# Moving the transposes, loads and sums of a seven-product matmul to other places in its written order

## The chip, the cores and the metric

The kernel runs on one core of a Trainium2 chip. The metric is device time in microseconds (us) of one execution, the median of several runs. One more execution is recorded by the hardware profiler; every duration below comes from that one.

## The reference

`x` has 8 x 1024 rows of 768 numbers. Each row is divided by its root mean square, scaled by `gamma`, and multiplied with a 768 x 2304 weight:

```python
rms = np.sqrt(np.mean(x ** 2, axis=-1, keepdims=True) + eps)
x_norm = x / rms * gamma
return np.matmul(x_norm, w_qkv).astype(np.float32)
```

## The kernel before

The 8192 rows are 64 tiles of 128 rows, called t. The first four tiles (t = 0 to 3) go through a plain bf16 matmul (`mm`, 512 columns at a time) while the weight is still arriving. The other 60 tiles form 30 pairs p = 2 to 31 (t = 2p and 2p+1). A pair is computed with a seven-product scheme in place of eight: the pair's rows and the two halves of the 768 inner numbers make a 2 x 2 of blocks (a11, a12, a21, a22), the weight is cut the same way (b11 to b22) in three column pieces c = 0, 1, 2 of twice 384 columns, and seven block products per piece, of sums and differences of blocks, give the four result blocks. A product (`product`) is three matmuls of 128 x 128 by 128 x 384.

For each tile there is a fixed chain of steps:

- `load_x`: the sync engine (SP) issues the load of 384 KB into one of 10 buffers.
- `pstat`, `prms`: ScalarE (ACT) squares and sums the row, then takes the root. `precip`: VectorE (DVE) takes the reciprocal.
- `pcast`: DVE scales the tile and writes it as f16 (line 626), into one of 6 buffers.
- `pxbar`: SP issues a DMA that transposes the f16 tile into one of 10 buffers `xT` (line 630).
- `osum`: four sums of blocks per pair (line 644), written to one tile `su` of a pool of three buffers. From pair 15 on they are all on GpSimd (POOL). A block of `su` is the stationary operand of four of the seven products.
- `product` on TensorE (PE, line 664), then `hold` (ACT or DVE, lines 671 and 673) copies a partial result from PSUM, `join` (DVE, line 680) adds a partial result to PSUM and writes an output block, `last` (ACT, line 684) writes the fourth output block.
- `rstore`: SP issues the store of one finished output row tile of 1152 KB (line 516).

Nothing is scheduled by a compiler. Each step gets a time, all steps are sorted by it, and they are emitted in that order; an engine executes its own steps strictly in the emitted order, each waiting only for the data and the buffers that it needs. The times therefore set only the order. SP has one queue for loads, transposes and stores alike, so a store that waits for its last `last` holds up the transposes behind it.

The order has two parts. The head is a list written out by hand or by a search (`PLAN`, 959 entries, pairs 2 to 14 and the plain matmuls); its times come from a planner's costs. The regular part (pairs 15 to 31) is a loop: `z` is the time of the pair's first product of a piece, and each step stands at `z + u * SLOT`, where `SLOT` is the time of one product (0.4875 us) and a pair takes 21 of these steps. Here a step of the beat is always such a slot; a negative `u` lies ahead of the pair's first product.

Of the kernel before, what the change touches and what calls it, by code (L numbers as in the profile page):

```python
# [15 lines left out]
HEAD_END = 164.41  # L16
# [11 lines left out]
    (10.183, "mm", 1, 0, "4"), (12.005, "conv", 1, 2, "POOL"), (12.006, "load_w", 7), (12.007, "load_w", 5),  # L28
    (12.008, "conv", 0, 1, "DVE"), (12.009, "mm", 0, 0, "5"), (12.010, "bound", 0, 1, "ACT"),
    (12.011, "mm", 0, 0, "4"), (12.012, "mm", 0, 0, "3"), (12.013, "load_w", 8), (12.014, "conv", 0, 0, "ACT"),  # L30
    (12.015, "tr", 3), (12.016, "stat", 3), (12.085, "mm", 0, 0, "01"), (12.517, "mm", 1, 0, "01"),
    (12.949, "mm", 1, 0, "2"), (12.950, "load_w", 10), (12.951, "load_w", 9), (13.145, "bound", 0, 0, "ACT"),
    (13.146, "cp", 3, "DVE"), (13.147, "recip", 0), (13.365, "evac", 1, 0, "DVE"), (14.025, "conv", 6, 3, "DVE"),
    (14.026, "mm", 0, 0, "2"), (14.027, "load_x", 4), (14.513, "evac", 0, 0, "DVE"), (14.514, "conv", 6, 2, "POOL"),
    (14.515, "mm", 2, 0, "012"), (14.516, "mm", 3, 0, "012345"), (14.517, "load_x", 5), (15.173, "recip", 3),
    (15.323, "mm", 0, 512, "23"), (15.755, "mm", 2, 512, "23"), (15.756, "conv", 7, 5, "POOL"),
    (15.757, "conv", 7, 4, "ACT"), (16.186, "mm", 1, 512, "45"), (16.187, "evac", 2, 0, "DVE"),
    (16.618, "mm", 0, 512, "54"), (16.619, "conv", 5, 1, "ACT"), (16.620, "conv", 5, 0, "DVE"),
    (17.050, "mm", 1, 512, "23"), (17.051, "bound", 0, 2, "ACT"), (17.481, "mm", 1, 512, "01"),
    (18.579, "evac", 3, 0, "ACT"), (18.580, "mm", 3, 512, "01"), (18.581, "mm", 3, 512, "45"), (18.582, "load_w", 14),  # L40
    (19.179, "conv", 10, 4, "ACT"), (19.180, "load_w", 15), (19.181, "bound", 1, 0, "DVE"),
    (19.182, "mm", 3, 512, "23"), (19.183, "conv", 8, 0, "POOL"), (19.184, "fold", 0), (19.208, "bound_tr", 0),
    (19.819, "evac", 3, 512, "ACT"), (19.820, "mm", 0, 512, "01"), (19.821, "evac", 1, 512, "DVE"),
    (19.822, "conv", 8, 1, "POOL"), (19.823, "conv", 10, 5, "POOL"), (19.824, "load_w", 11), (19.825, "load_w", 13),
    (20.419, "evac", 0, 512, "ACT"), (20.420, "mm", 3, 1024, "01"), (20.421, "bound_top", 0),
    (20.422, "bound_all", 0), (21.383, "pstat", 4), (21.384, "mm", 1, 1024, "01"), (21.385, "mm", 1, 1024, "45"),
    (21.386, "mm", 3, 1024, "45"), (21.607, "mm", 2, 1024, "45"), (21.608, "conv", 9, 3, "DVE"),
    (21.609, "conv", 9, 2, "POOL"), (22.038, "mm", 2, 512, "01"), (22.470, "mm", 3, 1024, "23"),
    (22.471, "scales", 0), (22.902, "mm", 1, 1024, "23"), (22.903, "pstat", 5), (23.343, "evac", 3, 1024, "ACT"),
    (23.344, "quad", 0, "b12", "POOL"), (23.345, "bound", 1, 2, "DVE"), (23.346, "quad", 0, "b11", "POOL"),  # L50
    (23.347, "mm", 2, 1024, "01"), (23.765, "mm", 0, 1024, "45"), (24.197, "mm", 2, 512, "45"), (24.198, "prms", 2),
    (24.199, "conv", 14, 0, "ACT"), (24.200, "conv", 14, 1, "POOL"), (24.629, "mm", 0, 1024, "23"),
    (24.630, "load_w", 12), (24.631, "bound", 1, 1, "DVE"), (24.632, "load_x", 6), (24.633, "precip", 2),
    (25.060, "mm", 0, 1024, "01"), (25.061, "fold", 1), (25.062, "pcast", 4), (25.492, "bound_tr", 1),
    (25.493, "conv", 14, 2, "POOL"), (25.494, "tsum", 0, "t1", "DVE"), (25.612, "mm", 0, 2048, "012"),
    (26.153, "bound_top", 1), (26.154, "quad", 0, "b22", "ACT"), (26.155, "mm", 1, 2048, "012"),
    (26.156, "evac", 0, 1024, "ACT"), (26.267, "mm", 3, 2048, "012"), (26.373, "evac", 2, 512, "DVE"),
    (26.595, "mm", 2, 1024, "23"), (26.596, "conv", 15, 3, "ACT"), (26.597, "load_x", 7),
    (26.853, "conv", 15, 5, "ACT"), (27.026, "bound_all", 1), (27.283, "conv", 11, 0, "ACT"),
    (27.923, "conv", 13, 5, "ACT"), (27.924, "pcast", 5), (27.925, "conv", 11, 1, "POOL"), (27.926, "load_x", 11),  # L60
    (27.927, "evac", 1, 1024, "DVE"), (27.928, "conv", 15, 4, "POOL"), (27.929, "ptr", 4),
    (27.930, "conv", 13, 4, "POOL"), (27.931, "mm", 2, 2048, "012"), (27.932, "mm", 0, 2048, "345"),
    (28.161, "mm", 2, 2048, "345"), (28.493, "quad", 0, "b21", "POOL"), (28.494, "mm", 3, 2048, "345"),
    (28.495, "scales", 1), (28.816, "mm", 1, 2048, "345"), (28.817, "evac", 0, 2048, "ACT"), (28.818, "load_x", 15),
    (28.819, "evac", 2, 1024, "DVE"), (29.144, "ptr", 5), (29.453, "evac", 3, 2048, "DVE"),
    (29.504, "mm", 2, 1536, "45"), (29.505, "conv", 12, 2, "ACT"), (29.935, "mm", 1, 1536, "45"),
    (29.936, "load_x", 8), (29.937, "evac", 2, 2048, "ACT"), (30.367, "mm", 2, 1536, "01"), (30.368, "load_x", 14),
    (30.369, "conv", 12, 3, "POOL"), (30.370, "pcp", 4, "DVE"), (30.799, "mm", 3, 1536, "45"),
    (31.230, "mm", 2, 1536, "23"), (31.231, "quad", 1, "b22", "DVE"), (31.232, "load_x", 9),
    (31.662, "mm", 0, 1536, "23"), (31.663, "load_x", 10), (31.664, "quad", 1, "b12", "POOL"),  # L70
    (32.094, "mm", 3, 1536, "23"), (32.095, "pstat", 6), (32.096, "pstat", 7), (32.097, "prms", 3),
    (32.098, "bound", 2, 1, "DVE"), (32.863, "precip", 3), (32.864, "mm", 1, 1536, "23"),
    (32.957, "mm", 3, 1536, "01"), (32.963, "pcp", 5, "DVE"), (32.964, "quad", 1, "b21", "POOL"),
    (33.463, "pcast", 6), (33.464, "mm", 0, 1536, "45"), (34.273, "pcast", 7), (34.274, "evac", 2, 1536, "ACT"),
    (34.275, "quad", 1, "b11", "ACT"), (34.413, "pxbar", 6), (34.414, "evac", 3, 1536, "ACT"),
    (34.415, "product", 2, 0, 1), (34.713, "hold", 2, 0, "a", "p1", "ACT"), (34.823, "osum", 2, "s1", "DVE"),
    (34.824, "mm", 1, 1536, "01"), (35.143, "tsum", 0, "t2", "DVE"), (35.144, "mm", 0, 1536, "01"),
    (35.172, "product", 2, 0, 2), (35.859, "join", 2, 0, 0, 0, "b", "p1"), (35.860, "product", 2, 1, 2),
    (36.409, "evac", 1, 2048, "DVE"), (36.410, "pxbar", 7), (36.809, "tsum", 1, "t1", "DVE"),
    (36.810, "osum", 2, "s2", "POOL"), (37.513, "tsum", 0, "t3", "DVE"), (37.514, "load_x", 12),  # L80
    (37.515, "bound", 2, 0, "ACT"), (37.516, "product", 2, 1, 1), (37.517, "product", 2, 0, 5),
    (37.518, "product", 2, 0, 6), (38.213, "tsum", 1, "t2", "DVE"), (38.214, "bound", 2, 2, "ACT"),
    (38.913, "osum", 2, "s4", "DVE"), (38.914, "hold", 2, 1, "a", "p1", "ACT"), (38.915, "evac", 1, 1536, "ACT"),
    (39.233, "fold", 2), (39.234, "product", 2, 1, 5), (39.383, "osum", 2, "s3", "DVE"), (39.384, "product", 2, 1, 6),
    (39.541, "bound_tr", 2), (39.661, "product", 3, 1, 2), (39.703, "tsum", 1, "t3", "DVE"),
    (39.704, "hold", 2, 1, "c", "p5", "ACT"), (40.403, "bound_top", 2), (40.404, "product", 2, 1, 3),
    (40.623, "osum", 3, "s3", "DVE"), (40.624, "rstore", 2), (40.943, "osum", 3, "s1", "DVE"),
    (40.944, "hold", 2, 0, "c", "p5", "ACT"), (40.945, "product", 2, 0, 3), (40.946, "evac", 0, 1536, "ACT"),
    (41.141, "bound_all", 2), (41.403, "osum", 3, "s2", "POOL"), (41.404, "product", 3, 1, 1),
    (41.405, "tsum", 0, "t4", "DVE"), (41.406, "rstore", 1), (41.407, "hold", 2, 1, "a", "u2", "ACT"),  # L90
    (41.613, "hold", 2, 0, "a", "u2", "ACT"), (41.753, "product", 2, 1, 7), (41.963, "scales", 2),
    (42.253, "product", 2, 0, 7), (42.283, "join", 2, 1, 0, 1, "c", "u2"), (42.833, "hold", 3, 1, "a", "p1", "DVE"),
    (42.834, "product", 3, 0, 1), (42.835, "load_x", 18), (42.836, "pstat", 9), (42.933, "tsum", 1, "t4", "POOL"),
    (43.228, "product", 3, 0, 2), (43.383, "join", 2, 1, 0, 0, "b", "p1"), (43.716, "product", 3, 1, 6),
# [252 lines left out]
def kernel(  # L347
# [23 lines left out]
    P = 128  # L371
# [268 lines left out]
    def osum(p, q, eng):  # L640
        if p not in SUM:
            SUM[p] = sums.tile([P, 4, H, P], f16, name="su")
        x, y, op = SUMS[q]
        (nc.vector if eng == "DVE" else nc.gpsimd).tensor_tensor(out=block(p, q), in0=block(p, x), in1=block(p, y), op=op)  # L644
# [163 lines left out]
```

## Time and profile before

| what | value |
|---|---|
| median of 3 runs | 353.53 us (352.62 to 354.30) |
| the profiled execution: device time | 354.05 us |
| the profiled execution: span from first to last instruction | 352.3 us |
| PE busy | 339.6 us (96%) |
| DVE busy | 267.7 us (76%) |
| ACT busy | 242.8 us (69%) |
| POOL busy | 119.8 us (34%) |
| DMA, main queue, share of 16 engines | 100.0% |
| products on PE, one matmul by the profile | 326 ns, 1887 of them |

The 326 ns of a matmul are longer than its place in the pipeline: matmuls overlap. The distance from one start to the next is what counts on PE, and a stall is a start that comes later than that distance allows. Idle time that the profile shows before a matmul is counted from the modelled end of the one before it, and is therefore smaller than the time that PE lost.

### The profile page before, as it was taken

Reading aid. Unit: us, or ns where it says so; the run is one execution under the profiler, and the core shown is the slowest. Engines: PE = TensorE matmul, PEld = TensorE weight load, DVE = VectorE, ACT = ScalarE, POOL = GpSimd, SP = SyncE. Lnnn points to the kernel's source line nnn. Section 1 sums busy time; section 2 is a strip of 40 time slices with the busy share of each in tenths; the row PEclk is TensorE's granted clock in tenths of the full one; section 3 lists DMA queues with packets and bytes.
Section 4 is the critical chain, followed back from the end, with each engine's and each line's share of the span. In section 5 each row is a group of like instructions: output and inputs, shape, how many; then the busy total and the mean of one; then the engine's idle time right before and its main releaser. Section 6 shows DMA issues by size and latency. Waiting matters only on the chain.

```text
span 352.3 us, 6192 instructions
## 1 busy us (share of the span) xinstructions
PE 339.6 (96%) x2059; PEld 200.1 (57%) x2062; DVE 267.7 (76%) x500; ACT 242.8 (69%) x498; POOL 119.8 (34%) x132
## 2 busy tenths in 40 slices
PE   5899999999999999999999999999999999999995
PEld 2346456656665656656666666555656565665662
DVE  3799898978876886777677787787787778776663
ACT  4899989777665767767576767666766666664543
POOL 1277383226021143314440333443444314433400
PEclk9999999999999999999999999999999999999999
DMA  7999999999999999999999999999999999979867
GB/s 263 391 379 392 278 342 305 277 386 232 418 196 365 340 423 349 396 411 357 393 349 422 347 367 341 387 400 318 348 310 381 371 274 399 301 246 292 293 245 293
DMA packets 69981, 119.57 MB, mean 339 GB/s; under 512 B 48822, under 2 KB 50236, under 8 KB 62012
## 3 DMA queue, kind: packets, MB, share of 16 engines
q1 hardware_dynamic: 69792, 119.06, 100.0%
q8 instruction: 16, 0.26, 0.3%
q14 instruction: 17, 0.14, 0.1%
q10 hardware_dynamic: 156, 0.10, 0.1%
HBM read 32.25 MB, written 75.50 MB: 306 GB/s over the span
## 4 chain that ended last, share of the span: by engine, by line
PE 87%; DMA 5%; DVE 3%; issue 2%; ACT 1%; SPq 1%; DVEq 0%
PE pm L664 81%; PE pm L492 6%; DMA wq<-in_w_qkv_dram 2%; DMA out_dram<-ot 2%; DVE xb L626 1%; DVE ot L680 1%; ACT pp L673 1%; DVE wq L602 1%; SPq L413 0%; SPq L418 0%; PE pm L649 0%; ACT w_b L426 0%; PE pm L691 0%; DVE w_b L680 0%; DVE rstd L621 0%
## 5 line engine op out<-in xcount | busy, mean ns | idle before, releaser
L664 PE MATMUL pm<-wq,su 128*128 128x384 f16 x1080 | 203.5, 326 | 0.7 <-DVE wq L602 0.7
L673 ACT ACTIVATE pp<-pm,sc 128x384 f32<-128x384 f32 x209 | 117.1, 579 | 75.8 <-PE pm L664 70.1
L664 PE MATMUL pm<-wq,xT 128*128 128x384 f16 x807 | 159.3, 326 | 2.1 <-DVE ot L680 1.5
L664 PEld LDWEIGHTS <-su 128*128 128x128 f16 x1080 | 105.6, 98 | 71.0 <-DVE wq L602 1.1
L680 DVE SCALAR_TENSOR_TENSOR ot<-pm,sc,pp 128x384 f32<-128x384 f32 x165 | 97.2, 613 | 29.9 <-PE pm L664 22.7
L664 PEld LDWEIGHTS <-xT 128*128 128x128 f16 x807 | 78.7, 98 | 55.4 <-issue 3.4
L644 POOL TENSOR_TENSOR su<-xT 128x384 f16<-128x384 f16 x52 | 49.6, 954 | 175.1 <-DMA xT<-xb 110.3
L680 DVE SCALAR_TENSOR_TENSOR w_b<-pm,sc,pp 128x384 f32<-128x384 f32 x105 | 62.7, 612 | 11.4 <-PE pm L664 8.4
L671 DVE TENSOR_SCALAR pp<-pm,sc 128x384 f32<-128x384 f32 x61 | 37.5, 615 | 27.6 <-PE pm L664 27.4
L612 ACT ACTIVATE sq<-x_t 128x768 bf16<-128x768 f32 x60 | 50.2, 837 | 1.2 <-DMA x_t<-in_x_dram 1.0
L684 ACT ACTIVATE ot<-pm,sc 128x384 f32<-128x384 f32 x68 | 38.5, 576 | 16.6 <-PE pm L664 16.4
L626 DVE TENSOR_SCALAR xb<-x_t,rstd 128x768 f16<-128x768 f32 x60 | 41.8, 728 | 0.7
L644 POOL TENSOR_TENSOR su<-su,xT 128x384 f16<-128x384 f16 x25 | 24.1, 963 | 9.5 <-DVE su L644 7.7
L644 POOL TENSOR_TENSOR su<-xT,su 128x384 f16<-128x384 f16 x25 | 23.5, 940 | 9.3 <-DVE su L644 7.6
L492 PE MATMUL pm<-w_b,xT 128*128 128x512 bf16 (+1 forms) x117 | 24.9, 357 | 1.3 <-ACT w_b L426 1.0
L492 PEld LDWEIGHTS <-xT 128*128 128x128 bf16 x120 | 11.3, 98 | 12.0 <-issue 1.9
L428 POOL TENSOR_SCALAR w_b<-wq,g_sb 128x512 bf16<-128x512 f32 (+1 forms) x14 | 9.5, 682 | 16.2 <-DMA wq<-in_w_qkv_dram 16.2
L684 ACT ACTIVATE w_b<-pm,sc 128x384 f32<-128x384 f32 x21 | 12.1, 575 | 4.0 <-PE pm L664 4.0
L612 ACT ACTIVATION_READ_ACCUMULATOR sq<-x_t 128x1 f32 x60 | 11.6, 193 | 0.0
L616 ACT ACTIVATE rms<-ssq,eps_sb 128x2 f32<-128x2 f32 x30 | 8.7, 293 | 0.1
L596 POOL TENSOR_SCALAR wq<-w_b,inv 128x1152 f16<-128x1152 bf16 x7 | 8.5, 1223 | 0.0
L554 ACT ACTIVATE sq<-w_b 128x1536 bf16<-128x1536 bf16 x5 | 7.4, 1477 | 0.8 <-DVE w_b L424 0.7
(53 smaller groups left out, 90.0 us busy)
## 6 DMA issues: line engine op xcount, KB each, us to landing
out_dram<-ot SPq DMA_DIRECT2D x42, 1152.0 KB, 7.2
x_t<-in_x_dram SPq DMA_DIRECT2D x64, 384.0 KB, 7.8
out_dram<-w_b SPq DMA_DIRECT2D x20, 1152.0 KB, 7.7
wq<-in_w_qkv_dram SPq DMA_DIRECT2D x10, 512.0 KB, 9.6
wq<-in_w_qkv_dram SPq DMA_DIRECT2D x4, 256.0 KB, 6.6
xT<-xb SPq DMA_TRANSPOSE x58, 7.3
wq<-in_w_qkv_dram SPq DMA_DIRECT2D x2, 384.0 KB, 9.7
out_dram<-w_b SPq DMA_DIRECT2D x2, 384.0 KB, 3.8
```

The lines of the kernel that those rows point to most:

```text
L428: nc.gpsimd.tensor_scalar(out=o, in0=i, scalar1=g, scalar2=1.0, op0=mult, op1=mult)
L492: nc.tensor.matmul(out=PM[t, n0][:, :nl], lhsT=XT[t][:, ko, :], rhs=w_b[:, ko, n0:n0 + nl], start=(b == 1), stop=(b == KO))
L596: nc.gpsimd.tensor_scalar(out=o, in0=quad_view(c, q), scalar1=INV[c], scalar2=1.0, op0=mult, op1=mult)
L612: nc.scalar.activation(out=sq, in_=X[t], func=AF.Square, accum_out=SS[p][:, t % 2:t % 2 + 1])
L616: nc.scalar.activation(out=r, in_=SS[p], func=AF.Sqrt, scale=inv_k, bias=eps_sb)
L626: nc.vector.tensor_scalar(out=XB[t], in0=X[t], scalar1=SS[t // 2][:, t % 2:t % 2 + 1], scalar2=None, op0=mult)
L644: (nc.vector if eng == "DVE" else nc.gpsimd).tensor_tensor(out=block(p, q), in0=block(p, x), in1=block(p, y), op=op)
L664: nc.tensor.matmul(out=PB[k][:, :CW], lhsT=block(p, a)[:, ko, :], rhs=WQ[c, b][:, ko, :], start=(first and ko == 0), stop=(ko == KO // 2 - ...
L671: nc.vector.tensor_scalar(out=o, in0=pb, scalar1=SC[c], scalar2=None, op0=mult)
L673: nc.scalar.activation(out=o, in_=pb, func=AF.Copy, scale=SC[c], bias=0.0)
L680: nc.vector.scalar_tensor_tensor(out=result(p, c, i, j), in0=PB[p, c, bank][:, :CW], scalar=SC[c], in1=PART[p, c, held], op0=mult, op1=add)
L684: nc.scalar.activation(out=result(p, c, 1, 0), in_=PB[p, c, "a"][:, :CW], func=AF.Copy, scale=SC[c], bias=0.0)
```

## The change

The change has three parts.

The regular part: `pstat`, `prms`, `precip` and `pcast` of every pair move 21 steps (one pair) ahead. `load_x` moves from step -96.3 to -103.9 for even pairs and to -124.7 for odd ones. `pxbar` stays at about -33 for even pairs and moves from -33.1 to -54.1 for odd ones. Since pair p+1 begins 21 steps after pair p, the four transposes of an even pair and of the odd pair behind it now stand in a row, and so do their four loads.

The sums: from pair 14 on, `osum` of an even pair requests one tile of the pool `sums` that is never used, before it requests the one that it writes. The pool still has three buffers.

The head: from about the 60th entry on, the same steps stand in another order, and some are on another engine. On SP the first 17 entries are as before, on PE the first 20 (the first transposes and plain matmuls).

```diff
-HEAD_END = 164.41
+HEAD_END = 164.30
...
-    (12.949, "mm", 1, 0, "2"), (12.950, "load_w", 10), (12.951, "load_w", 9), (13.145, "bound", 0, 0, "ACT"),
-    (13.146, "cp", 3, "DVE"), (13.147, "recip", 0), (13.365, "evac", 1, 0, "DVE"), (14.025, "conv", 6, 3, "DVE"),
...
+    (119.291, "hold", 10, 0, "c", "p5", "ACT"), (119.292, "pxbar", 23), (119.293, "product", 10, 2, 3),
+    (119.840, "join", 10, 2, 0, 1, "c", "u2"), (119.841, "product", 10, 0, 3), (119.842, "prms", 14),
+    (119.843, "pxbar", 24), (119.844, "pxbar", 25), (119.845, "pxbar", 26), (119.846, "pxbar", 27),
...
     def osum(p, q, eng):
         if p not in SUM:
+            if p >= 14 and p % 2 == 0:
+                sums.tile([P, 4, H, P], f16, name="su")
             SUM[p] = sums.tile([P, 4, H, P], f16, name="su")
...
             if c == 0:
+                odd = p % 2
                 for i in range(2):
                     t = 2 * p + i
-                    when(-96.3 + 0.1 * i, load_x, t)
-                    when(-64 + 7 * i, pstat, t)
-                    when(-48.1 + 1.3 * i, pcast, t)
-                    when(-33.1 + 0.1 * i, pxbar, t)
-                when(-54.5, prms, p)
-                when(-48.3, precip, p)
+                    when((-103.9, -124.7)[odd] + 0.1 * i, load_x, t)
+                    when(-85 + 7 * i, pstat, t)
+                    when(-69.1 + 1.3 * i, pcast, t)
+                    when((-33.3, -54.1)[odd] + 0.1 * i, pxbar, t)
+                when(-75.5, prms, p)
+                when(-69.3, precip, p)
                 for i, q in enumerate(SUMS):
                     when(-15 + 0.01 * i, osum, p, q, "POOL")
```

## The prediction

> **What bounds the kernel now.** I read the page first, then PE's timeline, the chain of waits, and DVE, POOL and SP around each place where PE stood still.
>
> ```profile
> PE 339.6 (96%) x2059; PEld 200.1 (57%) x2062; DVE 267.7 (76%) x500; ACT 242.8 (69%) x498; POOL 119.8 (34%) x132
> ...
> q1 hardware_dynamic: 69792, 119.06, 100.0%
> ```
>
> PE is the bound, and the DMA engines are as full. So time can be won only where PE stands still, and DMA may become the bound. PE's timeline shows the stalls:
>
> ```profile
> 219.73 1.63 PE L664 MATMUL pm<-wq,su 128*128 128x384 f16 x9
> 221.88 1.14 PE L664 MATMUL pm<-wq,xT 128*128 128x384 f16 x6 [0.52 <-DVE ot L680]
> ```
>
> Nine products' matmuls take 9 x 0.1625 = 1.46 us from start to start (195.82 to 197.28 elsewhere), so the next was due at 221.19 and came at 221.88: PE lost 0.69. The same sum gives all stalls past the start: head 0.91 (ends 40.18), 0.42 (75.69), 0.54 (112.79), together 1.87; regular part 0.69 (221.88), 0.70 (232.81), 0.16 (263.67), 0.54 (294.98), together 2.09. After 12.87 us PE loses hardly anything else. DVE's timeline names the cause in the regular part, the two casts of a pair, slow and normal:
>
> ```profile
> 218.83 2.47 DVE L626 TENSOR_SCALAR xb<-x_t,rstd 128x768 f16<-128x768 f32 x2
> ...
> 250.92 1.15 DVE L626 TENSOR_SCALAR xb<-x_t,rstd 128x768 f16<-128x768 f32 x2
> ```
>
> and POOL's what ran beside the slow one:
>
> ```profile
> 218.78 0.91 POOL L644 TENSOR_TENSOR su<-xT 128x384 f16<-128x384 f16 x1 [5.78 <-DMA xT<-xb]
> 219.78 1.11 POOL L644 TENSOR_TENSOR su<-su,xT 128x384 f16<-128x384 f16 x1
> 220.96 1.11 POOL L644 TENSOR_TENSOR su<-xT,su 128x384 f16<-128x384 f16 x1
> ```
>
> Casts that meet sums take up to twice as long; the join behind them frees PE's bank too late. Four pairs of casts fit one line: 1.94 us cost PE 0.16, 2.32 cost 0.54, 2.47 twice 0.69, so the slack is 1.78 us. Whether they meet is chance: the sums start when a transpose lands (the bracket), 5 to 15 us after POOL's last work, while casts keep their place in the beat.
>
> SP's timeline shows the order that the change moves:
>
> ```profile
> 254.25 0.35 SPq L516 DMA_DIRECT2D out_dram<-w_b  x1
> 258.30 0.34 SPq L516 DMA_DIRECT2D out_dram<-ot  x1
> 258.70 0.93 SPq L413 DMA_DIRECT2D x_t<-in_x_dram  x2
> 259.74 4.42 SPq L630 DMA_TRANSPOSE xT<-xb  x2
> ```
>
> Loads stand directly ahead of the transposes, so their 768 KB pass first.
>
> [...] 0.62 us casts become 1.26 beside sums, and sums grow from 0.91 to 1.11 or 1.23. [...]
>
> **The change part by part.**
>
> *Arithmetic and bytes*: none removed or added. PE's floor, and the edges of the span, stay.
>
> *pstat, prms, precip, pcast*: moved by exactly 21 steps, so each keeps its place in the beat and ACT and DVE keep their load. Cost 0 while loads are in time. The earliest statistic comes at -85, its load at -103.9: 18.9 x 0.4875 = 9.2 us for a load that takes 7.8 to land in the page. With four transposes ahead on SP it is issued about 4 steps (2 us) late, with the transposes already through; ACT may wait 0 to 1 us, but its holds tolerate that: ACT is idle 31%. I take 0. The 6 cast buffers become all full for some 14 steps; 0 unless transposes land over 6 us late.
>
> *Transposes*: two per pair remain. Two cost SP 3.4 to 7.0 us now (4.42 above), so four take 8 to 11. Queued behind them: the even row's store, due 13 steps (6.3 us) later, and then the four loads. That store is late by 2 to 5 us. 8 output buffers against rows that live some 36 steps of 21 per two rows, 3.4 in use on average, hide it; the cover gone, it costs what the stall at 112.79 did, 0.54. Gain: transposes no longer follow two loads: 768 KB at the 418 GB/s of a full window (259 to 266) is 1.9 us, plus 1.0 of issue, so an even pair lands about 2.9 us sooner. [...]
>
> *The extra tile*: three requests per two pairs from three buffers. If buffers go round strictly, each pair writes the buffer of the pair two back and cannot start before its last sum product, step 24 of that pair, that is 18 ahead of its own first. Sums then fill steps 4 to 12 of each beat (four take 3.8 us, 7.7 steps); casts come at 14.9 to 17.3. They never meet. First use of a sum is step +1; the end at about -9 leaves 5 us. A wait on POOL delays nothing else: POOL has only sums here. Gain 0.69 + 0.70 + 0.16 + 0.54 = 2.09 us.
>
> *Head*: the same steps. In the list ACT has 199 entries for 202, DVE 253 for 254, POOL 61 for 57. Its three stalls (1.87) hang on single meetings: three weight differences in a row on DVE (2.09 us at 38.04), two joins (75.02), a store not landed (112.12). Another order loses these and finds others. The gain is at most 1.87, as likely a loss of as much; I take 0, and the planner's clock (0.11 earlier) as no measurement.
>
> Sum for the profiled execution: 354.05 - 2.09 = 351.96 (span 350.2). It lay 0.52 above the median, so the median to come is 353.53 - 2.09 = **351.4 us**.
>
> **The rivals.**
>
> *The tie catches only even pairs, and every odd pair's sums fall on the casts (slower).* If the pool hands out the buffer that has been free longest, the extra request takes it and puts it back at the end: the even pair gets the buffer of two back, the odd one a buffer long free. Its transposes land right behind the even pair's, its sums start as the even ones end, at step 12, and run to 20, over the casts at 14.9. There are 7 such beats with casts left (even pairs 14 to 26). At 0.69 each: 4.83 - 2.09 = +2.74, 356.3 us. It decides once a meeting costs over 2.09 / 7 = 0.30, casts of 2.08 us. For it: nothing on POOL but the tie holds an odd pair back. Against: four meetings in the trace (208.57, 261.15, 271.54, 292.08) cost 0 to 0.54.
>
> *The same, with mild meetings, or no tie at all.* Casts of 2.0 to 2.1 us cost about 0.3, 7 x 0.3 = 2.1: nothing gained, 353.5. So also if the extra request does nothing and sums still follow landings.
>
> *The head wins too.* All its stalls gone: 351.4 - 1.87 = 349.6. For: they are single events. Against: a new order has its own.
>
> *The head loses.* 2 us of new stalls: 353.5, more with late stores; each full row that waits costs 0.5.
>
> **How the numbers follow.** Main case 0.50 (351.4, own range 350.0 to 352.9: half of the head's 1.87 and a run's scatter of 0.8 combined); head wins too 0.15; nothing gained, by mild meetings or by the head, 0.23; slower 0.12. From 349.4 to 355.2 about two tenths are left out, most of it above. Half a per cent, about what a measurement here can tell from no change, is 1.77: faster is below 351.76. Of the main case 0.60 lies there, with the head's 0.15 makes 0.45, and 0.01 of the rest: 0.46. Slower, above 355.3: 0.11 of the rival and 0.02 of a bad head: 0.13. The rest, 0.41, is the same.
>
> **What would show it.** Right: casts of 1.15 us in all pairs past 180 us, sums in a fixed place, waiting for PE and not for a landing, no join stall past 180, SP with four transposes in a row and four loads. Wrong tie: every second pair's sums start within 0.1 us of the end of the pair before, and casts there last over 2 us. Wrong on loads: ACT's squares wait for DMA x_t. Wrong on stores: joins wait for DMA out_dram. Wrong on the head: PE's loss before 175 us differs from 1.87.

## The result, and the profile after

The changed kernel takes 367.85 us (median of 4 runs, 367.23 to 368.23) against 353.85 us before (4 runs): ratio 1.040, 95% interval 1.037 to 1.043. It is slower by 14.0 us; 351.4 us, a gain of 2.1, was predicted. The profiled execution has a span of 365.7 us (352.3 before). Here and below, ratios leave out executions over 1.5% above the fastest of their kernel, medians and ranges don't.

The lines of the page of the kernel after that answer to those shown of before:

```profile
PE 341.8 (93%) x2059; PEld 200.0 (55%) x2062; DVE 269.8 (74%) x499; ACT 242.2 (66%) x495; POOL 125.7 (34%) x136
...
q1 hardware_dynamic: 69792, 119.06, 98.0%
...
PE 57%; DMA 25%; DVE 7%; issue 4%; ACT 4%; SPq 2%; DVEq 0%; ACTq 0%
```

PE does the same 2059 matmuls and is busy for 2.2 us more; the rest of the 13.4 us is time in which it stands still. The last line is the chain of work that ended last: DMA has 25% of it where it had 5%. Two waits have grown, in the list of waits (us in total, times, longest):

```profile
ACT sq L615 <- DMA x_t<-in_x_dram: 10.6, 7, 2.3
DVE ot L685 <- DMA out_dram<-ot: 10.0, 8, 2.6
```

Before they were 1.0 (2 times) and 3.5 (4 times). The squares wait for rows of x, the joins for a buffer whose store hasn't landed.

**Where PE loses it.** As in the prediction, what each matmul starts later than 162.5 ns after the one before it is summed, here by stage of the span, with the matmuls at half rate (320 to 325 ns apart) in a column of their own. (The 162.5 ns are for 384 columns; matmuls of other widths count in proportion: in the profile of before those of 512, 256 and 192 columns mostly start 216, 109 and 82 ns apart.) All numbers are from PE's timeline:

| us lost | to 35 us | 35 to 120 | 120 to 178 | from 178 | half rate | all | span |
|---|---|---|---|---|---|---|---|
| before | 6.9 | 2.0 | 0.0 | 1.9 | 0.3 | 11.6 | 352.3 |
| after | 6.6 | 5.1 | 6.4 | 6.2 | 0.2 | 24.9 | 365.7 |

(The last stop, 0.4 in both, is in "all".) The sums differ by 13.3 us, the spans by 13.4: nothing is left to explain elsewhere. Of the 13.3, 3.1 lie between 35 and 120 us, 6.4 at the end of the head, and 4.3 in the regular part, where a gain of 2.1 was expected; the start and the half rate give 0.4 back.

**The regular part.** PE's timeline shows two stops in one beat:

```profile
211.02 1.14 PE L669 MATMUL pm<-wq,xT 128*128 128x384 f16 x6 [0.39 <-DVE ot L685]
...
215.01 1.14 PE L669 MATMUL pm<-wq,su 128*128 128x384 f16 x6 [1.39 <-ACT pp L678]
```

The larger one comes from ScalarE, whose timeline has

```profile
213.08 0.84 ACT L615 ACTIVATE sq<-x_t 128x768 bf16<-128x768 f32 x1 [2.32 <-DMA x_t<-in_x_dram]
...
215.69 0.58 ACT L678 ACTIVATE pp<-pm,sc 128x384 f32<-128x384 f32 x1 [0.74 <-PE pm L669]
```

A square waited 2.32 us for its rows, and a hold that frees a bank for PE stood in ScalarE's queue behind it. Why the rows were late is in SP's timeline:

```profile
195.44 10.71 SPq L633 DMA_TRANSPOSE xT<-xb  x4
206.55 0.34 SPq L519 DMA_DIRECT2D out_dram<-ot  x1
206.96 3.39 SPq L416 DMA_DIRECT2D x_t<-in_x_dram  x4
```

SP stood on four transposes for 10.71 us. The square's own place in the beat was 210.8 (its predecessor ended at 210.18 + 0.58), its load's place 18.9 steps or 9.2 us ahead of that, at 201.6. It was issued at 206.96, 5.4 us late, and took 6.10 us to land.

The smaller stop is the old one. Every second pair of casts still meets sums on DVE,

```profile
208.10 2.34 DVE L629 TENSOR_SCALAR xb<-x_t,rstd 128x768 f16<-128x768 f32 x2
220.44 1.15 DVE L629 TENSOR_SCALAR xb<-x_t,rstd 128x768 f16<-128x768 f32 x2
230.68 2.15 DVE L629 TENSOR_SCALAR xb<-x_t,rstd 128x768 f16<-128x768 f32 x2
```

and POOL's timeline shows why: sums of two pairs run in a row, from the moment a transpose lands.

```profile
228.33 0.91 POOL L649 TENSOR_TENSOR su<-xT 128x384 f16<-128x384 f16 x1 [13.41 <-DMA xT<-xb]
...
231.18 2.42 POOL L649 TENSOR_TENSOR su<-xT 128x384 f16<-128x384 f16 x2
...
235.54 0.91 POOL L649 TENSOR_TENSOR su<-xT 128x384 f16<-128x384 f16 x1
```

Of the 6.2 us past 178, the five stops with a late load are 4.2 (1.55, 0.45, 0.45, 0.39, 1.35), the four with a slow pair of casts 1.7 (0.56, 0.37, 0.29, 0.51).

**The end of the head.** SP's timeline, and DVE's beside it:

```profile
115.20 10.90 SPq L633 DMA_TRANSPOSE xT<-xb  x5
...
133.14 16.53 SPq L633 DMA_TRANSPOSE xT<-xb  x4
```

```profile
140.19 0.62 DVE L685 SCALAR_TENSOR_TENSOR ot<-pm,sc,pp 128x384 f32<-128x384 f32 x1 [2.59 <-DMA out_dram<-ot]
```

The chain of work runs through a store issued at 129.22 that took 13.56 us to land. Stores held back behind five transposes went out in a burst and shared the DMA engines with four more (busy share 0.99 at 392 GB/s from 128 to 145 us). The three stops from 140 to 144 us (3.5 us) follow such joins. The other large stop here, 1.9 us at 167, is a square that waited for rows: their load, issued at 153.16, took 12.28 us to land.

### The profile page after: what moved, and what is told of

It reads as the page before. It is cut to its first block, busy times and chain, and to the rows that moved or that the text cites. A ratio compares the mean times of both kernels' runs of the same rounds, so it can differ in the third digit from the quotient of the medians.

```text
span 365.7 us, 6177 instructions
## 1 busy us (share of the span) xinstructions
PE 341.8 (93%) x2059; PEld 200.0 (55%) x2062; DVE 269.8 (74%) x499; ACT 242.2 (66%) x495; POOL 125.7 (34%) x136
## 4 chain that ended last, share of the span: by engine, by line
PE 57%; DMA 25%; DVE 7%; issue 4%; ACT 4%; SPq 2%; DVEq 0%; ACTq 0%
PE pm L669 51%; DMA out_dram<-ot 12%; DMA x_t<-in_x_dram 12%; PE pm L495 6%; DVE ot L685 3%; DMA wq<-in_w_qkv_dram 2%; ACT pp L678 2%; DVE xb L629 1%; ACT ot L689 1%; DVE pp L676 1%; ACT sq L615 1%; SPq L519 1%; DVE w_b L685 1%; SPq L416 0%; SPq L421 0%
## 5 line engine op out<-in xcount | busy, mean ns | idle before, releaser
L649 POOL TENSOR_TENSOR su<-xT 128x384 f16<-128x384 f16 x54 | 52.4, 978 | 162.0 <-DMA xT<-xb 85.3
L629 DVE TENSOR_SCALAR xb<-x_t,rstd 128x768 f16<-128x768 f32 x60 | 43.2, 748 | 0.8
L649 POOL TENSOR_TENSOR su<-xT,su 128x384 f16<-128x384 f16 x27 | 27.3, 1013 | 10.8 <-DVE su L649 9.0
L649 POOL TENSOR_TENSOR su<-su,xT 128x384 f16<-128x384 f16 x25 | 23.7, 947 | 15.7 <-DVE su L649 14.0
L615 ACT ACTIVATION_READ_ACCUMULATOR sq<-x_t 128x1 f32 x60 | 11.6, 194 | 0.0
L599 POOL TENSOR_SCALAR wq<-w_b,inv 128x1152 f16<-128x1152 bf16 x8 | 10.9, 1372 | 0.9 <-ACT sq L615 0.5
L605 DVE TENSOR_TENSOR wq<-wq 128x1152 f16<-128x1152 f16 x11 | 9.1, 849 | 0.0
```

What stands on the lines that cost most here:

```text
L599: nc.gpsimd.tensor_scalar(out=o, in0=quad_view(c, q), scalar1=INV[c], scalar2=1.0, op0=mult, op1=mult)
L615: nc.scalar.activation(out=sq, in_=X[t], func=AF.Square, accum_out=SS[p][:, t % 2:t % 2 + 1])
L629: nc.vector.tensor_scalar(out=XB[t], in0=X[t], scalar1=SS[t // 2][:, t % 2:t % 2 + 1], scalar2=None, op0=mult)
```

## The experiments

"Loss" is that of the table above. One profile is one execution: the old head between 35 and 120 us lost 1.5 to 4.0 us over eight profiles of kernels that have it with whole stores, so a difference of under 2 us there is not read.

### One half of the change at a time

```diff
 newhead_oldreg: the list and HEAD_END of after, the loop and the sums of before
 oldhead_newreg: the list and HEAD_END of before, the loop and the sums of after
```

> The new head list with the regular loop of the kernel before. If the head's own order carries its loss (PE loses 10 us before pair 15 in the kernel after, 1.9 in the one before, mostly joins that wait for a stored row to land): 361 to 363 us. If the head loses because the regular loop's first loads and transposes are mixed into it in rows of four: within 2 us of 353.9.

> The head list of before with the new regular loop. If the regular part costs 4 us more than before by its own four-in-a-row (PE loses 6.2 us there against 2.1): 357 to 359 us. If the new regular loop also spoils the end of the head: 360 to 363.

The new head alone takes 362.6 us (362.2 to 364.0), ratio 1.025 (1.020 to 1.030): +9.1. The new loop alone takes 362.0 us (361.6 to 363.3), ratio 1.024 (1.019 to 1.029): +8.5. Neither half carries the loss alone. Together they cost less (14.0) than the sum, because both spoil the end of the head: there (120 to 178 us) the new head alone loses 4.5, the new loop alone 6.2, both 6.4, the kernel before 0.0. So of the new loop's cost, in the profiled execution some 6 us fall between 120 and 178 us and 3.2 (5.1 for 1.9) after it, less some 2 that the start and the stretch to 120 us give back.

### The tie of the sums

The extra request of a tile has no effect. A tile that nothing reads or writes takes no buffer: built without the two lines, the kernel after consists of the same instructions on the same buffers. A real tie gives the pair the tile of the pair two back:

```diff
-            if p >= 14 and p % 2 == 0:
-                sums.tile([P, 4, H, P], f16, name="su")
-            SUM[p] = sums.tile([P, 4, H, P], f16, name="su")
+            SUM[p] = SUM[p - 2] if p >= 17 else sums.tile([P, 4, H, P], f16, name="su")
```

> The kernel after with a sums tile that from pair 17 on really is that of the pair two back. If meetings of casts and sums cost the rest (0.26, 0.56, 0.37, 0.29, 0.51 us): 365.5 to 366.5, casts of 1.15 us in all pairs past 200 us, the waits of squares for loads as before. If late loads alone count: 367 to 368.5.

It takes 368.7 us (367.9 to 370.3), ratio 1.043 (1.038 to 1.048): no gain. POOL's timeline says why:

```profile
231.84 0.91 POOL L647 TENSOR_TENSOR su<-xT 128x384 f16<-128x384 f16 x1 [13.39 <-DMA xT<-xb]
...
234.69 2.42 POOL L647 TENSOR_TENSOR su<-xT 128x384 f16<-128x384 f16 x2
```

The bracket is the landing again, not PE. Four transposes land so late that the tie has long been open, so it can't move the sums. The casts still meet them.

### Loads ahead of the four transposes

```diff
-                    when((-103.9, -124.7)[odd] + 0.1 * i, load_x, t)
+                    when((-103.9, -124.7)[odd] - 13.7 * (p >= 18) + 0.1 * i, load_x, t)
```

> The kernel after with the four loads of pairs 18 to 31 moved 13.7 steps ahead, so that they stand on SP before the four transposes. If ScalarE's squares that wait for late loads cause the regular part's large stalls (1.55, 0.45, 0.45, 0.39, 1.35 us): 4 us less, 363 to 364.5, and no square waits for a load past 200 us. If the casts that meet sums are the cause: no change, 367 to 368.5.

It takes 370.6 us (369.5 to 372.5), ratio 1.048 (1.043 to 1.054), slower still. The squares' waits are gone (one of 2.0 us left), but casts now wait, in DVE's timeline:

```profile
213.47 0.62 DVE L629 TENSOR_SCALAR xb<-x_t,rstd 128x768 f16<-128x768 f32 x1 [2.50 <-DMA xT<-xb]
```

A cast waits for a cast buffer that a transpose is still reading: with casts 21 steps early, the six buffers are full when the transposes come later. Past 178 us the kernel loses 7.3. Putting the loads first only chose another wait.

### Early casts with transposes in twos

The old head, and the new loop with loads and transposes back in twos, so that the early squares and casts stand alone:

```diff
-                    when((-103.9, -124.7)[odd] + 0.1 * i, load_x, t)
+                    when(-103.9 + 0.1 * i, load_x, t)
-                    when((-33.3, -54.1)[odd] + 0.1 * i, pxbar, t)
+                    when(-33.1 + 0.1 * i, pxbar, t)
```

> The head of before and the regular loop of after with the transposes and the loads back in twos: squares, roots and casts stay 21 steps (10.2 us) earlier than before, the loads of both pairs stand 103.9 steps ahead of their pair, the transposes 33.1. If four transposes in a row are what costs the regular part its 8.5 us (the theory), this takes 353 to 355 us, the time before. If the early casts are (they meet the end of the head, or hold the input and cast buffers), it stays at 359 to 362 us.

358.2 us (357.5 to 359.5), ratio 1.012 (1.009 to 1.016): half of the loop's cost, between the two expectations. Past 178 us it loses only 0.9; there the early casts cost nothing. All of the cost is one stop, at 136 us. SP's and ScalarE's timelines:

```profile
121.66 11.93 SPq L630 DMA_TRANSPOSE xT<-xb  x2
133.64 1.04 SPq L413 DMA_DIRECT2D x_t<-in_x_dram  x2
```

```profile
138.78 0.84 ACT L612 ACTIVATE sq<-x_t 128x768 bf16<-128x768 f32 x1 [3.94 <-DMA x_t<-in_x_dram]
```

Two transposes of the head held SP for 11.9 us, as they did in the kernel before (9.6). There the square came 15.7 us after its load's place (96.3 - 64 steps), now 9.2 (103.9 - 85 steps), and the load went out at 133.64, 1.2 us ahead of the square's place. PE stood for 3.57 us and ran at half rate after it (another 1.7 us lost).

### The loads earlier still

Both with loads at -113 for all pairs, the second with the transposes four in a row:

```diff
-                    when(-103.9 + 0.1 * i, load_x, t)
+                    when(-113 + 0.1 * i, load_x, t)
```

> The early casts with transposes in twos (358.2 us measured), and the loads of the regular pairs a further 9.1 steps (4.4 us) ahead, so that at the end of the head they stand before the pair of transposes that held SP for 11.9 us, and not behind it. If the squares' wait for a late load is the whole of what the early casts cost, the stop of 3.7 us at 136 us goes and this takes 353.5 to 355 us. If the early squares and casts cost by themselves (they stand ahead of the holds and joins on ScalarE and VectorE), it stays at 357 to 359 us.

> The same with the transposes four in a row: against the run with twos and the same loads, this gives what four in a row cost in the regular part. If four hold SP for 9 to 11 us and push stores and loads, 3 to 5 us more than that run (357 to 359 us), with the waits for out_dram and the stops after 200 us of the kernel after; if the loads were the whole cause, the same time as that run within 0.5 us.

In twos: 357.9 us (355.2 to 359.7), ratio 1.009 (1.006 to 1.012). The squares no longer wait (0.5 us in all), yet the stop is still there, 5 us later and shorter. SP's timeline, and the join on DVE at which PE now stops:

```profile
121.44 1.00 SPq L413 DMA_DIRECT2D x_t<-in_x_dram  x2
...
123.54 12.91 SPq L630 DMA_TRANSPOSE xT<-xb  x2
136.54 0.53 SPq L516 DMA_DIRECT2D out_dram<-w_b  x1
```

```profile
142.91 0.62 DVE L680 SCALAR_TENSOR_TENSOR w_b<-pm,sc,pp 128x384 f32<-128x384 f32 x1 [2.63 <-DMA out_dram<-w_b]
```

The loads got ahead of the transposes; the transposes took a microsecond longer, and the store behind them became what is late. The first expectation fell: the load wasn't the cost, only its last carrier.

Four in a row: 360.7 us (358.9 to 364.4), ratio 1.016 (1.012 to 1.021). That is 0.7% more than in twos, 2.4 us, under the 3 to 5 expected; three runs carry this ratio, and its interval touches that of the twos. The squares' waits are back (4.6 us).

### The new loop only from pair 18 on

```diff
-                    when((-103.9, -124.7)[odd] + 0.1 * i, load_x, t)
+                    when((-103.9, -124.7)[odd] + 0.1 * i if p >= 18 else -96.3 + 0.1 * i, load_x, t)
-                    when(-69.1 + 1.3 * i, pcast, t)
+                    when(-21 * (p >= 18) - 48.1 + 1.3 * i, pcast, t)
...
```

(Squares, roots, reciprocals and transposes in the same way, on the old head.)

> The head of before and, for the first three regular pairs (15 to 17), its own times for loads, squares, casts and transposes; from pair 18 on the regular loop of after. So nothing is brought forward into the end of the head. If the regular change costs twice (about 5 us at the end of the head, about 3 us by four transposes in a row after it), this takes 356 to 358 us and the squares' waits of over 2 us up to 170 us are gone. If the whole cost sits at the end of the head, 353.5 to 355; if it is all in the steady loop, 360 to 362.

361.9 us (359.9 to 363.0), ratio 1.021 (1.015 to 1.027): as slow as the new loop from the start. That looks like "all in the steady loop", but the profile says otherwise. Past 178 us it loses 3.6, 1.7 more than before. Most of the rest is one stop at 158 us and the half rate after it. Of the two large stops of the new loop on the old head, at 135 and 160 us, the first went with the old times; the second stayed. SP's, ScalarE's and PE's timelines:

```profile
147.54 4.19 SPq L413 DMA_DIRECT2D x_t<-in_x_dram  x4
```

```profile
160.36 0.84 ACT L612 ACTIVATE sq<-x_t 128x768 bf16<-128x768 f32 x1 [2.47 <-DMA x_t<-in_x_dram]
```

```profile
162.29 1.12 PE L664 MATMUL pm<-wq,su 128*128 128x384 f16 x3 [3.40 <-ACT pp L673]
```

In both kernels it is the same square that waits, that of pair 18's first rows. Their load went out at 147.54 here and at 150.08 with the new loop from the start, and took 12.74 and 10.52 us to land (chain of work). The plan leaves it 9.2 us, from the load's place to the square's (its lead). In the kernel before, the loads of this stretch, all those that line 413 issues between 140 and 165 us, took as long to land:

```profile
L413 SPq DMA_DIRECT2D x_t<-in_x_dram x6: 422/554/1190, 143.4 to 160.0; - x6
...
DMA to landing us min/median/max: 8.4/9.3/13.3
```

Pair 18's two took 12.7 and 13.3 us there, and no square waited, since the plan left them 15.7. With early casts in twos the lead is 9.2 too, but there this square starts without a wait, at 160.63 us, and there is no stop at 160. So this stop is no price that a loop pays once for being moved ahead: it comes where a landing takes longer than the shortened lead. The stop at 135 us is the same lead met by a load that goes out late: the kernel before issues it no sooner (134.26), and its square comes at 145.2. The expectation that waits like these would go with the old times held for the first stop alone.

Why landings are that long here isn't measured. The DMA engines had a busy share of 1.06 and 0.99 in the two halves of the stretch from 150 to 160 us, at 428 and 403 GB/s (before: 1.05 and 1.06, at 434 and 294); that they are full is what fits. Shown is that each repair handed the wait to another DMA.

### The head: whose order is it?

The new list with SP's loads, transposes and row stores in the old order from 30 us on, and the counterpart. An entry was moved (by up to 10 us) only where it would have come before what it needs or after who needs it; for instance, in the first:

```diff
-    (119.292, "pxbar", 23), (119.843, "pxbar", 24), (119.844, "pxbar", 25), (119.845, "pxbar", 26), (119.846, "pxbar", 27),
+    (106.3265, "pxbar", 24), (109.3290, "pxbar", 25), (109.5405, "pxbar", 23), (120.3530, "pxbar", 26), (123.0080, "pxbar", 27),
...
```

> The head of after with the regular loop of before (362.6 us measured), but from 30 us on the loads, transposes and row stores go to SP's queue in the order of the head before; the other engines keep the new order. If the new order of SP's queue (loads and transposes ahead of row stores, five transposes in a row) makes the head lose 9 us, this takes 353 to 356 us and the joins' wait for out_dram falls from 9.2 us to under 4. If the other engines' new order does it, it stays at 360 to 363 us.

> The counterpart: everything of before, but from 30 us to the end of the head SP's queue has the order of after. If SP's order alone makes the head lose, this takes 360 to 363 us; if it is the other engines' order, 353 to 355 us; something between if the two only lose together.

Both take about 376.5 us (ratios 1.065, 1.058 to 1.072; 1.064, 1.060 to 1.068). Neither theory foresaw it. Each order of SP fits the other engines' order that came with it, and a mixture is worse than both. This says nothing about whose order loses the 9 us.

### The head: the row of five, and the stores

The first moves two of the five transposes behind the first store that waits for them. The second halves the stores of the first 24 tiles (the other half of these rows isn't written), and the third does the same to the kernel before:

```diff
-(119.845, "pxbar", 26), (119.846, "pxbar", 27),
+(125.3031, "pxbar", 26), (125.3032, "pxbar", 27),
```

```diff
-        nc.sync.dma_start(out=of[t * P:(t + 1) * P, :], in_=OUT[t])
+        n = N // 2 if t < 24 else N
+        nc.sync.dma_start(out=of[t * P:(t + 1) * P, :n], in_=OUT[t][:, :n])
```

> The head of after with the regular loop of before (362.6 us), and of the five transposes in a row that held SP for 12.2 us at 117 us the last two moved behind the first row store that waits for them. If that row of five makes the burst of late stores, the stop of 3.2 us at 139 us and the slow matmuls after it (2 us) shrink and this takes 357.5 to 360 us. If the stores are late because the DMA engines are full whatever the order, it stays at 361.5 to 363.5 us.

> The head of after with the regular loop of before (362.6 us), but the row stores of the first 24 tiles write only the first half of each row (the other half of those rows is not written). If the new head loses its time to stores that land late, the waits for out_dram up to 150 us go and this takes 353 to 356 us. If the new order of the engines' own work costs, 359 us or more remain.

> The control to the head of after with half stores (354.3 us): the kernel before with the row stores of the first 24 tiles halved in the same way (the other half of those rows is not written). If the old head loses almost nothing to late stores, this takes 351.5 to 353.5 us, 1 to 2 us below the kernel before, and what remains between the two heads is 1 to 3 us. If half stores would help any head by as much, it falls to 346 us or below, and the half stores say nothing about the new order.

The stop that the first was aimed at, in the new head alone, on PE and on DVE:

```profile
139.03 0.65 PE L667 MATMUL pm<-wq,su 128*128 128x384 f16 x3
142.68 0.65 PE L667 MATMUL pm<-wq,xT 128*128 128x384 f16 x3 [2.99 <-DVE ot L683]
143.16 1.85 PE L667 MATMUL pm<-wq,su 128*128 128x384 f16 x6
```

```profile
142.00 0.62 DVE L683 SCALAR_TENSOR_TENSOR ot<-pm,sc,pp 128x384 f32<-128x384 f32 x1 [4.48 <-DMA out_dram<-ot]
```

With the five split, 359.9 us (358.7 to 362.4), ratio 1.017 (1.012 to 1.021), as the first theory had it: 2.7 us of the 9 come back, and this stop becomes two of 0.90 and 1.27.

Half stores on the new head give 354.3 us (352.6 to 356.0), ratio 1.000 (0.998 to 1.002), and the waits for out_dram disappear from the list. On the old head the same edit gives 352.3 us (351.3 to 353.2), ratio 0.996 (0.994 to 0.997). So what the new head costs falls from 2.5% to 1.0001 - 0.9958 = 0.4%, from 8.7 us to 1.5. Some 7 us of the new head's loss hang on the bytes of these stores, and the old order avoids nearly all of that with the same stores. Whether the stores cost by landing late themselves or by slowing the rest isn't separated. Nor does a long row alone do it: the five at 117 us held SP for 12.16 us in the new head, and the old head has a longer one,

```profile
90.46 13.05 SPq L630 DMA_TRANSPOSE xT<-xb  x6
```

and PE has no stop there between 76 and 112 us. Which of the moved entries cost, besides the five transposes, stays open.

### Transposes earlier, and nothing else

If casts lose to sums that start when a transpose lands, an earlier transpose should part them. One number of the kernel before:

```diff
-                    when(-33.1 + 0.1 * i, pxbar, t)
+                    when(-40.9 + 0.1 * i, pxbar, t)
```

> The kernel before with one number changed: the two transposes of a regular pair stand 40.9 steps ahead of it instead of 33.1, so that they should land 3.8 us sooner, and the sums should be over before the next pair's casts. If casts that meet sums are what the regular part loses 2.09 us to, and the sums wait for the transposes, casts take 1.15 us in every pair and the time falls by 1.5 to 2.1 us, to 351.5 to 352.0. If the transposes only stand longer in the queue, or push the row stores behind them, the time stays within 0.5 us or rises by 1 to 3 us.

> The kernel before with the transposes of a regular pair 7.8 steps earlier, once more, against more runs of the kernel before: 0.9971 with 0.9943 to 0.9999 was measured. If the casts that no longer meet the sums are worth what the profile of it shows (1.5 to 2.1 us), the ratio is 0.994 to 0.996; if the head's own changes from run to run cover it, 0.997 to 1.000.

Faster, but by less than the 1.5 to 2.1 us expected: first 352.8 us (351.4 to 356.2), ratio 0.997 (0.994 to 0.9999); again, against 43 runs of the kernel before, 352.8 us, ratio 0.996 (0.994 to 0.998). DVE's timeline of the second run, in the beats where before had pairs of 1.81, 2.47 and 2.47 us:

```profile
209.93 1.15 DVE L626 TENSOR_SCALAR xb<-x_t,rstd 128x768 f16<-128x768 f32 x2
220.16 1.15 DVE L626 TENSOR_SCALAR xb<-x_t,rstd 128x768 f16<-128x768 f32 x2
230.40 1.15 DVE L626 TENSOR_SCALAR xb<-x_t,rstd 128x768 f16<-128x768 f32 x2
```

Past 178 us PE loses 0.3 and 1.0 in the two profiles, for 1.9 before; three quarters of the 1.0 follow a pair of casts that still met sums (the second of the two took 1.26 us, at 179.74). This is the version that beats both kernels, by 0.4%. It is less than the 0.5 to 0.6% that the regular part had to give, and the profiles don't say where the rest went: the head, untouched here, lost 1 to 2 us more than in the profile of before, which is within its scatter.

### The runs by stage

Left out are tie_real and loads_first, which lose in the places where the kernel after does, the first run of the earlier transposes, and the two mixtures of the head, which lose 13 us each between 35 and 120 us.

| us lost by PE | to 35 | 35 to 120 | 120 to 178 | from 178 | half rate | ratio |
|---|---|---|---|---|---|---|
| before | 6.9 | 2.0 | 0.0 | 1.9 | 0.3 | 1 |
| after | 6.6 | 5.1 | 6.4 | 6.2 | 0.2 | 1.040 |
| newhead_oldreg | 5.9 | 5.8 | 4.5 | 2.9 | 1.1 | 1.025 |
| newhead_split5 | 6.6 | 4.3 | 3.1 | 2.9 | 0.3 | 1.017 |
| newhead_halfst | 7.8 | 2.4 | 0.9 | 2.3 | 0.0 | 1.000 |
| before_halfst | 5.0 | 1.1 | 0.0 | 1.5 | 0.2 | 0.996 |
| oldhead_newreg | 5.3 | 1.5 | 6.2 | 5.1 | 0.0 | 1.024 |
| twos_cast_early | 5.6 | 1.7 | 3.8 | 0.9 | 1.7 | 1.012 |
| twos_loads_early | 5.3 | 2.5 | 2.3 | 1.1 | 1.7 | 1.009 |
| fours_loads_early | 6.0 | 2.4 | 4.0 | 2.5 | 1.6 | 1.016 |
| newreg_from18 | 5.9 | 3.2 | 4.0 | 3.6 | 1.4 | 1.021 |
| xbar_again | 5.6 | 3.0 | 0.1 | 1.0 | 0.2 | 0.996 |

## Why the prediction was wrong, step by step

*"PE is the bound, and the DMA engines are as full. So time can be won only where PE stands still, and DMA may become the bound."* Right, and the part that decided was then left out of the sum. Every step after it priced a moved DMA by its own lateness and looked for a cover; none asked what a full queue does with work that is brought forward.

*"It is issued about 4 steps (2 us) late ... I take 0."* This is the first step that failed. The four transposes took 10.71 us on SP, inside the 8 to 11 given (though the 3.4 to 7.0 for two that it rests on is read from the regular part: at the end of the old head two held SP for up to 9.75 us); against the 6.5 us of plan between transposes and loads that alone is 4 us, and the measured lateness was 5.4. The lead of 9.2 us had 1.4 to spare over the landing of 7.8 that the step itself named (the loop before had 15.7). The cover, "ACT is idle 31%", doesn't cover: what counts is what stands behind the waiting square in ScalarE's queue, a hold that PE needs. A wait of 2.32 us cost PE 1.55. In the steady loop this is 4.2 us.

*The same step, at the end of the head.* "Moved by exactly 21 steps, so each keeps its place in the beat": true past 178 us (early casts in twos lose 0.9 there). But the loads of even pairs moved by only 7.6 steps, so their lead fell from 15.7 to 9.2 us, and the 7.8 set against it is the median of all loads. At the end of the head loads of the kernel before took up to 13.3 us to land, and one went out behind two transposes that held SP for 9.63 us. The old lead covered both; the new one doesn't, which gives the stops at 135 and 160 us, 2.8 and 2.7 us. The step was in the sum, with the landing of another stage.

*"That store is late by 2 to 5 us. 8 output buffers ... hide it; the cover gone, it costs ... 0.54."* Right for the regular part, where no join waits past 178 us. In the head, where the same argument wasn't made, the buffers are all out: eight waits, up to 2.59 us each, and one stop of 3.2 us in the new head alone, six times the price given.

*"An even pair lands about 2.9 us sooner."* Wrong. Its sums start at step 10 of the odd pair's beat. Four transposes stay four transposes: the two pairs land together (from 204.7 to 208.3 us in the row issued at 195.44), and the sums of both run in a row over the casts of every second beat.

*"If buffers go round strictly ... Gain 2.09."* The tie doesn't exist, as "no tie at all" among the rivals allowed; and a real one changes nothing, since the landing comes later than it. What this gain rested on, that casts lose to sums, is right as far as it was measured (in the profile of before casts of 0.62 us take up to 1.28 beside sums; why isn't shown): with the transposes earlier nearly all slow pairs are gone and so are nearly all stops past 178 us.

*"Head ... I take 0", at most 1.87 either way.* Mis-sized by a factor of five: +9.1. The three stalls of the old head were read as the scale of what an order can lose. They are what is left once an order fits; the mixtures, at +22.6 us, show what one that doesn't fit costs.

*The rivals.* The slower one foresaw the pattern, slow casts in every second pair, by another mechanism (the tie catching only even pairs) and at 0.69 a meeting; they cost 0.29 to 0.56. "The head loses" was the right rival with 2 us in place of 9. The signs named for wrong loads, wrong stores and a wrong tie all appeared. The range ended at 355.2 since each of them was priced at the size of one known stall and none at that of a full queue.

## What to carry to other kernels

When the queue of DMAs is full (100.0 and 98.0% of the 16 engines' span in the profiles of before and after), price a transfer that is moved by what then stands behind it. Give a load a lead for the landing of its own stage, not for the median (here 7.8 us against up to 13.3). A late input costs what is queued behind the instruction that waits for it, whatever the idle share of that engine (here a wait of 2.32 us on an engine that is idle 34% of the span cost PE 1.55). And small stops in a tuned order don't measure what another order may lose; to win those few, move one thing (here the transposes, by 8 steps, for 0.4%).

## What the runs showed of the hardware

After some stops PE ran at half rate for 2 to 4 us. In the new head alone, after the stop of 2.99 us shown above, the stretch from 142.7 to 147.1 us has (busy us of the engines, then granted clock, DMA share, GB/s)

```profile
142.70:147.10 4.40, 4.01 (x16) 1.91 (x16) 2.64 (x5) 0.54 (x1) 0.00 (x0) 0.61 1.02 431
```

There are 16 matmuls where 27 fit: six start 320 ns after the one before, for 162.5, and a stop of 0.76 us lies among them. The same followed stops of 3.40 (newreg_from18) and 3.57 us (twos_cast_early). A stop of 2.01 us (twos_loads_early, at 143) was followed by it too, with a granted clock of 0.62 from 144 to 148 us, while one of about 2.6 us (oldhead_newreg, at 136) and three in a row of 1.59, 0.41 and 1.02 (after, at 140) were not: the clock was 1.00 from 139 to 143 us in the one and from 142.7 to 147.1 in the other. So the length of a stop alone doesn't tell; where the half rate came, it cost 1.1 to 1.7 us more in the runs of the table. Nor is it the same in every execution: the mean granted clock of the kernel after was 0.997 in the profiled one and 0.988 to 0.991 in the other three.

Transposes on SP were the other surprise: in the profile of before a pair of them held the queue for 2.60 us early in the head (at 55.96) and for 9.63 us at 123.95, and in twos_loads_early one held it for 12.91 us, at 123.54. The busy share of the DMA engines doesn't tell the two of before apart: 0.99 at 420 GB/s in the one, 1.03 at 429 in the other. What differed is what was still under way when they were issued: one store and one load in the first, four stores and two loads in the second. That is two cases, not a rule; but here the price of a transpose couldn't be taken from another stage.
